# Two attention stages of a two-layer diffusion block rewritten as loops over cycles, with own rooms for weights and modulation loads

## The chip, the cores and the metric

The kernel runs on one core of one Trainium2 chip. TensorE (PE) multiplies matrices, VectorE (DVE), ScalarE (ACT) and GpSimd (POOL) work on rows of numbers, and SyncE (SP) issues most transfers. The metric is device microseconds (us) of one execution, as the median of several timed runs. Beside the timed runs there is one profiled execution with its trace; all views of the profile come from it.

## The reference, cut to what matters

Two trunk layers run on 256 context tokens and 512 latent tokens of width 1024, in fp32. Layer 0 mixes tokens by differential attention, layer 1 by neighbourhood attention with a learned bias. Each is followed by a squared-ReLU MLP, and each half is shifted, scaled and gated by six vectors of 1024 that come from `silu(c) @ w_mod`.

```python
for i in range(DEPTH):                                   # DEPTH = 2
    mod_l = split(silu(c) @ w_mod[i] + b_mod[i], 6)      # mod_c likewise from c_ctx
    h_l = modulate(rms_norm(x, norm1_g[i]), mod_l[0], mod_l[1])
    h_c = modulate(rms_norm(ctx, norm1_g[i]), mod_c[0], mod_c[1])
    # layer 0, 8 heads, two q/k maps of 64 each; latents read context + latents, context reads context
    #   s = q @ k.T / 8;  p = softmax(s);  w = p[map 0] - lam * p[map 1];  o = rms_norm(w @ v) * (1 - lam_init)
    # layer 1, 16 heads of 64; a latent reads the context and a window of 8 rows x 16 columns
    #   p = softmax([s_window + bias, s_context]);  o = p @ v
    x = x + mod_l[2] * (o @ w_o)
    x = x + mod_l[5] * (square(relu(modulate(rms_norm(x), mod_l[3], mod_l[4]) @ w_mlp1[i])) @ w_mlp2[i])
    # context tokens: the same with mod_c, in layer 0 only
```

## The kernel before, in words

The 768 tokens are six tiles of 128: tiles 0 and 1 are context, 2 to 5 latent. A product of two fp32 numbers is made of three passes over parts that are rounded to a shorter form (`PASSES`: high by high, and both mixed ones). So a weight that is loaded into a raw buffer `R` (two buffers, `wload`, L110) is first copied by ACT into the high half of a tile `W` (L118), and then POOL subtracts that from the raw value into the low half (L119). A matmul on `W` waits for both.

The stages follow each other on PE: a first head whose projection is merged with the first modulation chunks; layer 0's attention; its output projection; the MLP; layer 1's attention in eight groups of two heads; its output projection; the MLP. In an attention stage PE's instructions are not reordered: they stand as the text of the kernel issues them (`tc.manual_schedule`). The other engines and SP are ordered by a scheduler, each in a fixed order of its own, and every queue is worked off in that order.

**Layer 0's attention.** A head has these steps: the projection of six tiles, each in two half steps of twelve 128x384 matmuls (`qkv0`, L375); the turning of rope-rotated q and k (L453); scores (L499), softmax (L504, L505 and the blend L511), turning of the softmax weights (L523 and the copies L525, L526), the product with v (L534), and the turning of its output (L487, L488). Tables of letters, `ORD_HEAD` and its kind, say in which order generators are stepped: `q` the projection of the next head, `a` the attention of this one, `b` the first scores of the next, `z` the tail of the one before, `l`, `m` and `n` load, begin and end of a modulation chunk (eight 32x256 matmuls, L224, and a few small ones). At a head's end `b q a` puts two half steps of the last tile, the next head's scores of tile 0, and this head's last turn one behind the other. The first head of the loop runs by `ORD_HEAD0`, after a first head that is not in it. At its end `ORD_OUT0` weaves the last head's attention with the output projection over seven heads; the eighth follows whole (`while not last`).

**Rooms.** `sbuf_phase` opens a set of tile rooms that is closed as a whole: "s0" (five `W` of 1024 columns), "sA" (eight `W` of 768), "sB" (five of 1024) and so on. Modulation loads are two halves of 512 KB through `R` in the attentions, and one of 1 MB in a `W` room elsewhere. Of 48 chunks 8 are in the first head, 17 in layer 0's attention, 19 beside layer 0's MLP and 4 (`MODS_LATE`) in layer 1's attention.

**Layer 1's attention** is built alike: `qkv1` projects (L375), `attend1` does scores (L642), softmax, turning (L667) and product (L683), ordered by `ORD_FIRST1`, `ORD_GROUP`, `ORD_GROUP7` and `ORD_OUT1`. The projection of a group runs beside the attention of the one before; the first group's projection stands alone at the start.

Of the kernel before, what the change touches and what calls it, by code (L numbers as in the profile page):

```python
# [35 lines left out]
ORD_HEAD0 = "l qqqq a q a q a m aa q n a q aa q a l a q aa m aa q n aaa q a q aa b q a"  # L36
ORD_HEAD = "a q z a q z aa q z p q l a q aa q m l q a q a n q aa m aa q n aa q aa qq aa b q a"
ORD_OUT0 = "l a z a m z a n z q l p a a m a a n q a a q aa l aa q m aa q aa q n aa q a qq a q a q a Q"
ORD_FIRST1 = "qqqqqqqqqqqq rr q r a"
ORD_GROUP = "q a qq a qq aa q a q aa q a q r a r q a r a b"  # L40
ORD_GROUP7 = "l q a qq a qq aa q a q aa q a q m a n q a a b"
ORD_OUT1 = "q a l a m a n l aa m a n q aa q a q a qq a l m n Q"

MODS_LATE = 4


ATT0 = ((0, 1), (1, 0), (2, 0), (1, 1), (2, 1), (0, 2), (3, 0), (0, 3), (1, 2), (3, 1), (2, 2), (0, 4), (1, 3),
        (3, 2), (2, 3), (0, 5), (1, 4), (3, 3), (2, 4), (1, 5), (2, 5), (3, 4), (3, 5))
ATT1 = ((0, 1), (1, 0), (2, 0), (0, 2), (1, 1), (2, 1), (0, 3), (1, 2), (2, 2), (1, 3), (2, 3))
# [9 lines left out]
class Block:  # L59
    def __init__(self, tc, ctx, a):  # L60
# [9 lines left out]
        self.room = {}  # L70


    BUFS = {"H": 8, "Q": 8, "E": 2, "X": 2, "Y": 6, "O": 4, "T": 2, "SQ": 12, "SA": 12, "SO": 8, "V": 1, "C4": 1}

    def sbt(self, tag, shape, dt=F32):
        self.n += 1
        pool, bufs = (self.room[tag], self.bufs[tag]) if tag in self.room else (self.sb, self.BUFS[tag])
        return pool.tile(shape, dt, tag=tag, name=f"{tag}{self.n}", bufs=bufs)

    @contextmanager  # L80
    def sbuf_phase(self, name, wcols, **tags):

        with ExitStack() as st:
            self.wcols, self.bufs = wcols, tags
            self.room = {tag: st.enter_context(self.tc.tile_pool(name=name + tag, bufs=n, reuse_waits="tile"))
                         for tag, n in tags.items()}
            yield
# [22 lines left out]
    def wload(self, src, n, tile=None, eng=None):  # L110
# [5 lines left out]
        if w is None:  # L116
            w = self.sbt('W', [P, 2, self.wcols], F32R)
# [213 lines left out]
    def first_head(self, xnT, mods):  # L331
# [8 lines left out]
        def modulate_pair(kp):  # L340
            for _ in range(2):
                mods.load(True)
            w[kp] = self.wload(self.a["wqa"][0, kp], 768)
# [368 lines left out]
    def project(self, l, wo, oT, last, t0, xsrc, tag_o, tag_h, tag_p, out):  # L712
# [43 lines left out]
        while not last:  # L756
            yield
# [308 lines left out]
```

## Time and profile before

| what | us |
|---|---|
| three timed runs | 2003.57, 1999.56, 2001.33 (median 2001.33) |
| profiled execution, its own time | 1994.66 |
| its span in the profile | 1992.5 |
| PE busy in the span | 1826.0 (92%) |
| DVE, ACT, POOL busy | 1174.4, 808.4, 793.1 (59%, 41%, 40%) |

By the trace the stages lie at these times from the span's start: the first head to 65.9 us, the first two heads of the loop to 205.4, the next four to 437.4, the last to 490.4, the end of layer 0's attention with the first part of its output projection to 577.5, the rest of that projection and layer 0's MLP to 1206.4, the first group of layer 1 to 1247.3, six groups to 1501.1, the last group with the first part of the output projection to 1595.3, and layer 1's MLP to the end.

The profile is read by stage. Its windows view has one row for a stretch: from and to, its length, then busy time and number of instructions of PE, PEld (weight loads of PE), DVE, ACT and POOL, then the clock that PE was granted (1.00 is full), the share of time in which the transfer engines were busy, and GB/s. A row of the timeline is a run of like instructions: start, length, engine, line, operation, output and inputs, shapes, count, and in brackets the idle time ahead of it and what ended it. A row of the chain of waits has start, length, engine and what ran.

### The profile page before, as it was taken

To read this page: it belongs to the slowest core of one execution; us is meant where nothing else is said; L and a number is where in the kernel's file an instruction comes from. 1 tells how busy PE (TensorE), PEld (TensorE's weight loads), DVE (VectorE), ACT (ScalarE), POOL (GpSimd) and SP (SyncE) were. 2 spreads that over 40 slices of the span, in tenths; PEclk is the share of its full clock that TensorE was granted. 3 is DMA by queue.
4 is the path that set the end of the run, shared out by engine and by line. 5 is a ranking of instruction groups with operands and counts; after the bars stand their busy time and mean duration, and the time that the engine had idled before them with its cause. 6 is when DMAs were issued, how large, how long until landed. Compare 5 with 4: busy or idle time off the path is not lost.

```text
span 1992.5 us, 27095 instructions
## 1 busy us (share of the span) xinstructions
PE 1826.0 (92%) x10256; PEld 1592.5 (80%) x10256; DVE 1174.4 (59%) x2191; ACT 808.4 (41%) x1819; POOL 793.1 (40%) x684
## 2 busy tenths in 40 slices
PE   6689888898889999999999988889897889999998
PEld 5678787887668888888899978888887678888886
DVE  4577767777656433433434686777778564444446
ACT  4465656566525212212222244555566342322231
POOL 3644545544422212222323444445443234443443
PEclk9799999999899999999999998999999889999999
DMA  7211211213523323323321132222323423332332
GB/s 292 70 54 67 83 67 61 83 43 125 167 74 117 98 93 127 127 92 125 112 64 64 52 102 69 54 54 62 75 61 122 138 75 95 96 106 85 95 97 72
DMA packets 59441, 185.00 MB, mean 93 GB/s; under 512 B 7408, under 2 KB 13872, under 8 KB 55856
## 3 DMA queue, kind: packets, MB, share of 16 engines
q1 hardware_dynamic: 53568, 173.44, 28.0%
q10 hardware_dynamic: 5744, 9.85, 1.3%
q8 instruction: 80, 1.31, 0.3%
q14 instruction: 49, 0.40, 0.1%
HBM read 174.45 MB, written 8.81 MB: 92 GB/s over the span
## 4 chain that ended last, share of the span: by engine, by line
PE 68%; DVE 15%; ACT 6%; DMA 4%; issue 4%; POOL 2%; SPq 0%; ACTq 0%; POOLq 0%; DVEq 0%
PE PD L800 21%; PE PA L375 11%; PE PA L835 10%; PE PB L835 9%; PE PA L729 4%; PE PS L499 2%; PE PA L224 2%; PE PB L534 2%; PE PB L683 1%; PE PQ L365 1%; DVE SA L504 1%; ACT E L505 1%; ACT W L118 1%; DVE N L278 1%; DMA R<-in_wqb_dram 1%
## 5 line engine op out<-in xcount | busy, mean ns | idle before, releaser
L119 POOL TENSOR_TENSOR W<-R,W 128x1024 fp32r<-128x1024 f32 (+1 forms) x200 | 452.0, 2268 | 686.3 <-ACT W L118 648.2
L118 ACT ACTIVATE W<-R 128x1024 fp32r<-128x1024 f32 (+1 forms) x204 | 199.7, 995 | 460.3 <-PE PB L835 357.1
L800 PE MATMUL PD<-Q,W 128*128 128x384 f32 (+1 forms) x1584 | 291.3, 334 | 1.2 <-DVE Q L300 0.7
L800 PEld LDWEIGHTS PD<-Q,W 128*128 128x128 f32 x1584 | 271.8, 188 | 13.4 <-issue 4.9
L375 PE MATMUL PA<-W,H 128*128 128x384 f32 x1008 | 210.7, 360 | 10.3 <-DVE Q L431 5.0
L375 PEld LDWEIGHTS PA<-W,H 128*128 128x128 f32 x1008 | 186.9, 203 | 16.2 <-issue 5.2
L809 DVE TENSOR_TENSOR N<-N 128x768 f32<-128x768 f32 (+1 forms) x64 | 63.6, 997 | 223.9 <-ACT N L805 117.6
L800 PE MATMUL PD<-H,W 128*128 128x512 f32 (+1 forms) x816 | 183.9, 382 | 3.4 <-DVE H L301 2.5
L800 PEld LDWEIGHTS PD<-H,W 128*128 128x128 f32 x816 | 149.2, 192 | 32.8 <-DVE H L301 2.7
L375 PE MATMUL PA<-W,Q 128*128 128x384 f32 (+1 forms) x1008 | 172.8, 325 | 2.2 <-ACT H L411 2.2
L835 PE MATMUL PA<-W,H 128*128 128x512 f32 x648 | 165.4, 395 | 3.0 <-DVE T L841 2.7
L375 PEld LDWEIGHTS PA<-W,Q 128*128 128x128 f32 x1008 | 159.1, 192 | 2.4 <-ACT H L411 2.4
L263 POOL TENSOR_TENSOR SQ<-SQ,half 128x4 f32<-128x4 f32 (+1 forms) x96 | 92.7, 968 | 167.9 <-DVE SQ L386 158.8
L835 PEld LDWEIGHTS PA<-W,H 128*128 128x128 f32 x648 | 119.4, 188 | 30.6 <-issue 4.5
L835 PE MATMUL PB<-W,H 128*128 128x512 f32 x504 | 129.6, 391 | 0.0
L835 PE MATMUL PA<-W,Q 128*128 128x512 f32 x432 | 110.4, 395 | 2.2 <-ACT Q L811 1.6
L835 PEld LDWEIGHTS PB<-W,H 128*128 128x128 f32 x504 | 94.3, 188 | 18.6
L499 PE MATMUL PS<-Q,Q 128*128 128x256 f32 (+1 forms) x320 | 72.2, 360 | 30.7 <-ACT E L505 27.4
L835 PEld LDWEIGHTS PA<-W,Q 128*128 128x128 f32 x432 | 81.2, 188 | 22.1 <-ACT Q L811 2.4
L846 DVE TENSOR_TENSOR H<-PA,H 128x512 f32<-128x512 f32 x78 | 53.6, 688 | 70.9 <-PE PA L835 70.9
L504 DVE TENSOR_REDUCE SA<-PS 128x1 f32<-128x768 f32 (+1 forms) x96 | 74.5, 776 | 27.9 <-PE PS L499 14.4
L505 ACT ACTIVATE E<-PS,SA 128x768 f32<-128x768 f32 (+1 forms) x96 | 72.8, 759 | 39.2 <-DVE SA L504 39.2
(218 smaller groups left out, 3144.9 us busy)
## 6 DMA issues: line engine op xcount, KB each, us to landing
R<-in_w_dram SPq DMA_DIRECT2D x128, 512.0 KB
W<-in_wmod_dram SPq DMA_DIRECT2D x27, 1024.0 KB
R<-in_wmod_dram SPq DMA_DIRECT2D x42, 512.0 KB
R<-in_wqa_dram SPq DMA_DIRECT2D x32, 384.0 KB
R<-in_wqb_dram SPq DMA_DIRECT2D x32, 384.0 KB
X<-in_rpb_dram SPq DMA_DIRECT2D x48, 128.0 KB
R<-in_woa_dram SPq DMA_DIRECT2D x8, 512.0 KB
R<-in_wob_dram SPq DMA_DIRECT2D x8, 512.0 KB
```

Of the source, the lines that this page charges most:

```text
L118: nc.scalar.activation(w[:, 0, :n], raw, AF.Copy)
L119: (eng or nc.gpsimd).tensor_sub(w[:, 1, :n], raw, w[:, 0, :n].bitcast(F32))
L263: nc.gpsimd.tensor_tensor(r, ss, self.half[:, :n], op=ALU.pow)
L375: nc.tensor.matmul(acc[:, :n], hT[kt][:, x, P * i:P * i + P], w[kt // 2][:, y, o:o + n], start=(kt == 0 and p == 0), stop=(kt == KT - 1 an ...
L499: nc.tensor.matmul(s[:, c0:c1], q[:, m, P * i:P * i + P], k[:, m, c0:c1], start=p == 0, stop=p == 1)
L504: nc.vector.tensor_reduce(mx, s, op=ALU.max, axis=AX, negate=True)
L505: nc.scalar.activation(e[:, m, :nk], s, AF.Exp, bias=mx[:, 0:1], accum_out=sm[:, m:m + 1])
L729: nc.tensor.matmul(ps, oHL[h][:, x, c:c + P], w[h // 2][:, y, 512 * (h % 2):512 * (h % 2) + 512], start=(first and h == hs[0] and p == 0), ...
L800: nc.tensor.matmul(ps[:, at:at + b1 - b0], w[kt // 4][:, x, o:o + P], hT[kt][:, y, b0:b1], start=(kt == 0 and p == 0), stop=(kt == KT - 1 ...
L809: nc.vector.tensor_mul(r, r, r)
L835: nc.tensor.matmul(ps, hd[:, x, P * i - c0:P * i - c0 + P], w[f][:, y, 512 * n:512 * n + 512], start=(f == 0 and p == 0), stop=(f == len(h ...
L846: nc.vector.tensor_add(av, ps, av)
```

## The change

Both attentions become loops over cycles. `head0` and `group1` return a function of a letter and a number: `Q` a projection step, `U` a turn of q and k, `S` scores, `T` the turning of softmax weights, `V` the product with v, `O` the turning of an output. A string per cycle says the order; a step without a mark is of head c, with one mark of head c-1, with two of head c-2. `run` reads it. The steps issue the operations that they issued before. In layer 0 the cycle of head c holds its projection, the attention of c-1 and the last products and outputs of c-2. `START0` weaves heads 0, 1 and 2; `END0` the rest of heads 6 and 7 with the output projection over six heads (`P`; `X` loads and splits the seventh), in two half steps of nine matmuls for a tile; heads 6 and 7 follow in `end`, six matmuls for a tile in place of three. In layer 1 the cycle of group c holds its projection and the attention of c-1.

```diff
-ORD_HEAD = "a q z a q z aa q z p q l a q aa q m l q a q a n q aa m aa q n aa q aa qq aa b q a"
+CYCLE0 = """Q0a O2'' n1' S1' O3'' V4'' V5'' U4' Q0b Q1a T0' T1' Q1b O4'' S2' V0' Q2a O5'' Q2b S3' T2' U0 Q3a V1' O0'
+Q3b S4' T3' Q4a Q4b V2' O1' m0 S5' T4' U2 n0 Q5a V3' Q5b m1 S0 T5'"""
+START0 = """Q0a' Q0b' Q1a' Q1b' Q2a' S0'' Q2b' S1'' Q3a' U0' T0'' Q3b' T1'' Q4a' V0'' V1'' Q4b' S2'' U2' Q5a' O0''
+S3'' T2'' Q5b' O1'' m0 Q0a V2'' S4'' T3'' n0 Q0b U4' O2'' V3'' S5'' T4'' m0 Q1a O3'' V4'' n0 Q1b S0' T5''
...
+END0 = """O2'' n1' S1' O3'' V4'' V5'' m0 T0' U4' T1' n0 O4'' V0' S2' O5'' P0a V1' X6 P0b O0' S3' T2' P1a O1' P1b
+S4' T3' P2a V2' P2b m1 S5' T4' P3a V3' O2' n1 P3b T5' P4a V4' O3' P4b V5' O4' P5a P5b O5'"""
-ORD_GROUP = "q a qq a qq aa q a q aa q a q a r q a r q a r a b"
+CYCLE1 = """Q0 S0' Q1 Q2a S1' T0' Q2b Q3a S2' T1' Q3b Q4a U0 V0' S3' Q4b Q5a T2' Q5b V1' T3' U2 V2' U4 V3'"""
+END1 = """S0' S1' T0' S2' T1' P2a V0' S3' P2b T2' P3a V1' P3b T3' P4a X6 V2' P4b P5a V3' P5b"""
-MODS_LATE = 4
@@ sbt: a tag with several rooms goes round over their buffers
+            pools = [r[:2] for r in self.room[tag] for _ in range(r[1])]
+            k = self.turns[tag] = self.turns.get(tag, -1) + 1
+            pool, bufs = pools[k % len(pools)]
@@ mod_load
-            w = self.sbt('W', [P, 2048])
+            w = self.sbt('M', [P, 2048])
@@ head0, the first head's tile step
-            eng = nc.vector if accs and i in (2, 4) else nc.gpsimd
+            eng = nc.vector if accs and i in (2, 4, 5) else nc.gpsimd
@@ head0, output(i): one tile and one transfer for two output tiles
-        if last is None:
-            nc.scalar.dma_start(self.oT0[h], oTs[0])
+            if i % 2 == 1:
+                if split:
+                    split(oTs[j], j)
+                else:
+                    nc.scalar.dma_start(self.oT0[h][:, 256 * j:256 * j + 256], oTs[j])
@@ project
-            split(st, nc.vector if h % 3 == 0 and h else nc.gpsimd)
+                split(h, nc.gpsimd if h % 3 == 2 else nc.vector)
@@ hybrid_block
+        mod = {"m": lambda _: (mods.begin(), mods.load(True)), "n": lambda _: mods.end()}
+        b.open("left", WA=4)
+        b.open("right", N=2, M=3)
...
+            b.close("M", "N")
+            b.open("right", M=1, O=4, OT=2, WB=4)
...
+            def after(h):
+                if h + 2 < HEADS0:
+                    w[h + 2] = b.load_qkv(a["wqa"], h + 2, ("WA", "WB")[h % 2])
+                elif h + 2 == HEADS0:
+                    b.close("WA")
+                    b.open("left", W=3)
+                    proj.update(b.project(0, a["woa"], b.oT0, 0, lambda i: xs[i], 'H', 'Q', 'S', done))
+                    for k in range(3):
+                        proj["weights"](k)
+                else:
+                    b.close("WB")
+                    b.open("right", N=4, W=1)
+                    proj["begin"]()
...
+                for c in range(2, HEADS0):
+                    heads[c] = b.head0(c, w[c], hT, split=proj.get("split_last"), then=lambda c=c: after(c))
+                    run(START0 if c == 2 else CYCLE0, c, heads, **mod)
@@ sideB, called twice in an iteration of layer 0's MLP
-                if len(mods.todo) > MODS_LATE:
-                    mods.load(True)
-                    mods.chunk()
+                mods.chunk()
+                mods.load(True)
@@ layer 1
-        ph.enter_context(b.sbuf_phase("sC", wcols=768, W=6, N=4))
+        b.open("left", W1=6)
+        b.open("right", VM=2, N=4)
...
+                for c in range(GROUPS1):
...
+                    run(CYCLE1, c, heads)
+                b.close("W1")
+                b.open("left", W=4)
```

`WA` holds the weights of even heads and `WB` those of odd ones, four tiles each; the load for head h+2 is issued behind head h's last projection step (`then`), into the same room. A modulation load in layer 0's attention and MLP is one transfer of 1 MB into the only buffer of `M`, issued behind the chunk that used it. The MLPs have four `W` in place of five. Of the 48 chunks 8 are in the first head, 16 in layer 0's attention (4 in `START0`, two in each of five cycles, 2 in `END0`), 24 beside layer 0's MLP and none in layer 1's attention.

The rows below show three places, first of the kernel before, then of the change. Each row is an instruction (or a run of like ones): the line, what it is, output, inputs and shape. The lines of `wload` are L118 and L119 before, L127 and L128 now.

PE at the end of a cycle of layer 0: `PS` are score banks, `PA` projection banks, `PB` banks in which softmax weights `E` are turned, `Q` the head's q and k, `H` the tokens.

```order
L499 MATMUL PS_2782<-Q_2206,Q_2204 128x256
L375 MATMUL PA_2741<-W_1500,H_460 128x384 x3
L375 MATMUL PA_2741<-W_1500,H_467 128x384 x3
L375 MATMUL PA_2741<-W_1505,H_549 128x384 x3
L375 MATMUL PA_2741<-W_1505,H_556 128x384 x3
L523 MATMUL PB_2826<-ident,E_2689 128x128 x3
L523 MATMUL PB_2832<-ident,E_2689 128x128 x3
L499 MATMUL PS_2860<-Q_2205,Q_2204 128x256
```

```order
L233 MATMUL PA_3463<-M_3323,silu 32x256 x8
L493 MATMUL PS_3478<-Q_3137,Q_3136 128x256
...
L517 MATMUL PB_3495<-ident,E_3325 128x128 x3
L517 MATMUL PB_3501<-ident,E_3325 128x128 x3
L384 MATMUL PA_3507<-WB_2772,H_321 128x384 x3
L384 MATMUL PA_3507<-WB_2772,H_328 128x384 x3
L384 MATMUL PA_3507<-WB_2777,H_374 128x384 x3
L384 MATMUL PA_3507<-WB_2777,H_381 128x384 x3
L545 MATMUL PB_3521<-ident,O_3302 128x128
L248 MATMUL PA_3463<-sel,T_3472 128x2 x2
L493 MATMUL PS_3529<-Q_3137,Q_3136 128x256
```

Before, the six turns of tile 5 stand between the scores of tile 0 (`PS_2782`) and of tile 1 (`PS_2860`) with nothing else; now a chunk's matmuls stand ahead of the first scores (`PS_3478`), and twelve projection matmuls of the next head, an output turn and the chunk's small matmuls between the turns and the second scores (`PS_3529`).

ACT at the start of the output projection: `E` are exponentials, the rows `H<-N` the copies of head outputs that come back from memory, `OT` (`N<-PB` before) the outputs of the last heads.

```order
L505 ACTIVATE E_5728,SA_5729<-PS_5730,SA_5739 128x768
L235 DMA gates<-T_5755 2x256
L721 ACTIVATE H_5627<-N_5625 128x768
L721 ACTIVATE H_5632<-N_5630 128x768
L505 ACTIVATE E_5728,SA_5729<-PS_5730,SA_5742 128x768
L721 ACTIVATE H_5642<-N_5640 128x768
L721 ACTIVATE H_5647<-N_5645 128x768
L721 ACTIVATE H_5657<-N_5655 128x768
L505 ACTIVATE E_5779,SA_5780<-PS_5781,SA_5790 128x768
```

```order
L519 ACTIVATE X_5548<-PB_5549 128x384
L519 ACTIVATE X_5548<-PB_5555 128x384
L717 ACTIVATE H_5480<-N_5478 128x768
L499 ACTIVATE E_5530,SA_5531<-PS_5532,SA_5537 128x256
L717 ACTIVATE H_5485<-N_5483 128x768
L546 ACTIVATE OT_5561<-PB_5562,subg 128x128
L717 ACTIVATE H_5490<-N_5488 128x768
L499 ACTIVATE E_5530,SA_5531<-PS_5532,SA_5540 128x256
L717 ACTIVATE H_5495<-N_5493 128x768
```

Before, the copies stand beside the exponentials of a latent tile (128x768); now they begin beside those of a context tile (128x256), one ahead of the first and two ahead of the second of its exponentials.

POOL between two groups of layer 1: `SQ` is the power for the norm of q and k, `X<-X,C` the bias with its mask, `H` copies of k, `VM` copies of v.

```order
L119 TENSOR_TENSOR W_11898<-R_11896,W_11898 128x768
L263 TENSOR_TENSOR SQ_12083<-SQ_12081,half 128x4
L119 TENSOR_TENSOR W_11903<-R_11901,W_11903 128x768
L572 TENSOR_TENSOR X_12878<-X_12878,C_6651 128x256
L119 TENSOR_TENSOR W_12403<-R_12401,W_12403 128x768
L572 TENSOR_TENSOR X_12878<-X_12878,C_6651 128x256 x5
L119 TENSOR_TENSOR W_12408<-R_12406,W_12408 128x768
L263 TENSOR_TENSOR SQ_12172<-SQ_12170,half 128x4
```

```order
L272 TENSOR_TENSOR SQ_12742<-SQ_12740,half 128x4
L573 TENSOR_TENSOR X_13178<-X_13178,C_6649 128x256
L128 TENSOR_TENSOR W_12390<-R_12388,W_12390 128x768
L573 TENSOR_TENSOR X_13178<-X_13178,C_6649 128x256
L128 TENSOR_TENSOR W_12395<-R_12393,W_12395 128x768
L573 TENSOR_TENSOR X_13178<-X_13178,C_6649 128x256 x2
L620 CAST VM_12874<-H_12423 64x256
L272 TENSOR_TENSOR SQ_12793<-SQ_12791,half 128x4
L128 TENSOR_TENSOR W_12895<-R_12893,W_12895 128x768
```

Between two powers (to `SQ_12172` before, to `SQ_12793` now) there stood three weight subtractions and six mask additions, and now stand two subtractions, four additions and a copy of v.

More of the change, by code (lines that the diff above doesn't have):

```diff
@@ L779, in mlp @@
+        return dict(weights=weights, begin=begin, split=split, step=step, split_last=split_last, end=end)
     def mlp(self, l, t0, xh, hT, tag, mid, done, side):
@@ L885, in chunk, with run @@
         self.end()
[L888 to L902 removed]
+def run(order, c, steps, **others):
+    for word in order.split():
+        kind, num, h = word[0], word[1:].rstrip("'"), c - word.count("'")
+        if kind in others:
+            others[kind](num)
+        elif h in steps:
+            steps[h](kind, 2 * int(num[0]) + (num[1:] == "b") if kind == "Q" else int(num))
 def hybrid_block(tc, a, out):
```

388 lines of the change are left out of this document (174 added, 214 removed).

## The prediction

> **What bounds the kernel now.** I read the page first, then the windows by stage, then PE's timeline and the chain of waits at the end of a head.
>
> ```profile
> span 1992.5 us, 27095 instructions
> PE 1826.0 (92%) x10256; PEld 1592.5 (80%) x10256; DVE 1174.4 (59%) x2191; ACT 808.4 (41%) x1819; POOL 793.1 (40%) x684
> ```
>
> PE bounds the whole, but 92% is a mean. The windows (from and to, length, busy PE, PEld, DVE, ACT, POOL, granted clock, transfer share, GB/s) show where it stands:
>
> ```profile
> 65.90:205.40 139.50, 108.97 (x639) 96.69 (x639) 99.25 (x205) 78.77 (x218) 79.10 (x93) 0.87 0.22 71
> 205.40:437.40 232.00, 204.88 (x1310) 187.23 (x1308) 167.03 (x379) 139.92 (x407) 114.21 (x152) 0.94 0.21 70
> 437.40:490.40 53.00, 50.12 (x341) 44.03 (x342) 38.58 (x95) 32.55 (x99) 22.44 (x35) 1.00 0.29 97
> 490.40:577.50 87.10, 67.73 (x329) 51.44 (x327) 55.61 (x100) 40.12 (x91) 33.29 (x23) 0.84 0.44 144
> 674.30:1004.20 329.90, 329.90 (x1848) 286.29 (x1849) 127.33 (x169) 70.84 (x91) 88.09 (x37) 1.00 0.34 113
> 1206.40:1247.30 40.90, 38.48 (x244) 38.00 (x243) 22.06 (x59) 17.46 (x52) 20.00 (x25) 0.94 0.23 53
> 1247.30:1501.10 253.80, 227.11 (x1549) 218.65 (x1550) 192.74 (x442) 149.20 (x395) 119.31 (x141) 0.98 0.25 61
> 1501.10:1595.30 94.20, 77.09 (x444) 60.43 (x442) 65.48 (x128) 45.57 (x102) 30.16 (x23) 0.87 0.42 135
> ```
>
> In the MLP (674.30) PE is never idle. In the attentions it stands, and at less than the full clock. Four heads take 232.00, so 58.0 each; the fifth takes 53.00 at clock 1.00 with 50.12 busy. The gap lies at a head's end (timeline, then two pieces of the chain, then a window):
>
> ```profile
> 376.12 2.55 DVE L511 SCALAR_TENSOR_TENSOR E<-E,SA 128x768 f32<-128x768 f32 x1
> 378.73 0.93 PE L523 MATMUL PB<-ident,E 128*128 128x128 f32 x6 [0.72 <-DVE E L511]
> 383.35 1.23 PE L499 MATMUL PS<-Q,Q 128*128 128x256 f32 x4 [3.69 <-ACT E L505]
> 438.72 0.74 PE L499 MATMUL PS<-Q,Q 128*128 128x256 f32 x4 [2.73 <-ACT E L505]
> 384.57 3.84 PE PA L375 x12
> 390.42 2.10 PE PA L375 x12
> 326.40:330.20 3.80, 3.80 (x13) 3.80 (x13) 3.52 (x8) 1.49 (x5) 2.98 (x3) 0.50 0.30 102
> ```
>
> The scores of tile 1 wait 3.69 until the exponentials of tile 0 have emptied the only score bank; behind that the next twelve matmuls take 3.84 in place of 2.10, and the window of the same place a head earlier has clock 0.50. After the wait of 2.73 the clock stays at 1.00 (window 437.40). So a head of 58.0 loses some 7 in waits and slow clock. The Trainium skill's "TensorE: Matmul & The Clock Gate", section "What's actually happening", has the clock at half or full, falling after an idle window of about 3.4 us; the two waits agree with it, and it would bring the penalty back with any wait that long.
>
> **The change, part by part.**
>
> *Steady cycles of layer 0.* The matmuls stay; their order moves. The work of a head at full clock is 50.12, less a third chunk that this window holds (1.00 + 0.55 by the two rows below, about 1.4 in it): 48.7. This is the floor of a cycle.
>
> ```profile
> 785.17 1.00 PE PA L224 x16
> 790.24 0.55 PE PA L230 x2
> 503.12 3.79 DMA R<-in_wmod_dram
> ```
>
> Between the scores of tiles 0 and 1 now stand twelve projection matmuls (2.10) and the turns, and ahead of tile 0's a chunk (1.00). The wait of 3.69 goes down to nearly nothing, and the half clock behind it with it (3.84 − 2.10 = 1.7). What is late next: the softmax of tile 5, whose blend L511 takes 2.55 where POOL's weight subtraction runs beside it, and ACT, which still has weight copies among the exponentials.
>
> ```profile
> L511 DVE SCALAR_TENSOR_TENSOR E<-E,SA x48: 473/1018/2551, 96.4 to 543.1; 128x768 f32<-128x768 f32 x32, 128x256 f32<-128x256 f32 x16
> L118 ACT ACTIVATE W<-R 128x768 fp32r<-128x768 f32 x60 | 49.7, 849 | 32.6 <-DMA R<-in_wqb_dram 22.0 <-DMA R<-in_wqa_dram 7.7 <-DVE SA L257 2.0
> L119 POOL TENSOR_TENSOR W<-R,W 128x768 fp32r<-128x768 f32 x60 | 110.7, 1849 | 48.6 <-issue 36.3 <-ACT W L118 12.2
> ```
>
> I leave 3.3 for waits per cycle, bounded by 0 (all hidden) and 9.3 (a head as slow as now); 3.3 is near the 2.9 that the 53.00 window idles, plus half of one weight copy (0.85). A cycle is 52.0; four of them gain 4 × 6.0 = 24.0. The fifth has 48.7 + 2.9 = 51.6, gain 1.4. The Trainium skill's "SBUF — State Buffer", section "Who interferes with whom", has a DVE instruction with two SBUF inputs and a GpSimd one that reads SBUF shut each other out; the 2551 against a median of 1018 agrees. By it the blend stays slow wherever a weight subtraction meets it, some 1.5 us a cycle, and the sum would be 6 less in gain.
>
> *Loads.* A chunk's load is now 1 MB, issued when the chunk before it has been used, since `M` has one buffer. The row above has 512 KB in 3.79, so two are 7.6. From `m0` to `m1`, the narrower window of a cycle, stand two half steps (2 × 2.10) and a set of scores, a product and two sets of turns, an estimate of 9 us with 1.5 to 1.7 for each of the first two; from `m1` round to `m0` the rest of the cycle, some 40. In the MLP the window at 674.30 holds nine iterations with two chunks' places each: 329.90/18 = 18.3, less the 1.00 of the matmuls, about 17.5. So 7.6 is hidden everywhere; without that cover each load costs what it is late by (the last rival). SP waits at this load, and the weight loads behind it wait too: those of head h+2 are issued a head ahead, in rooms of their own, so nobody stands for them. The per-pair output transfers (three for one) are on ACT's queue and small; 0.
>
> *Start.* Three heads merged replace two loop heads of 139.50. Its waits:
>
> ```profile
> 67.42 0.44 PE L375 MATMUL PA<-W,H 128*128 128x384 f32 x1 [1.51 <-ACT W L118]
> 70.01 3.94 PE L375 MATMUL PA<-W,H 128*128 128x384 f32 x11 [2.14 <-POOL W L119]
> 76.39 1.32 PE L375 MATMUL PA<-W,H 128*128 128x384 f32 x6 [1.63 <-POOL W L119]
> 80.55 1.11 PE L453 MATMUL PA<-ident,Y 128*128 128x128 f32 x4 [2.85 <-DVE Y L445]
> 92.25 0.66 PE L453 MATMUL PA<-ident,Y 128*128 128x128 f32 x2 [3.79 <-ACT W L118]
> 98.16 4.18 PE L375 MATMUL PA<-W,H 128*128 128x384 f32 x12 [3.97 <-DVE Q L431]
> ```
>
> Two cycles of work with their residue are 2 × 52.0 = 104. The waits for weights (1.51 + 2.14 + 1.63 = 5.3) come before any attention can fill them and stay. Of the other three (10.6) half stays, since the rope of tile 5 moves to DVE and more heads are there to weave: 5.3. For slow clock I add 3. Together 118, gain 21.5 (bounds: 5, with all waits as before, to 35, with none).
>
> *End of layer 0's attention.* 87.10 now.
>
> ```profile
> 577.47 14.16 PE L729 MATMUL PA<-W,H 128*128 128x512 f32 x61 [0.37 <-DVE T L734]
> 508.98 5.62 DMA N<-oT
> ```
>
> A matmul of 128x512 is 14.16/61 = 0.232. Twelve half steps of nine are 25.1, the last two heads' 36 are 8.4 (18 more than before), and a cycle without its projection (144 matmuls of 2.10/12, 25.2) is 23.5: work of 57. The copies of the six heads' outputs now stand among the exponentials of tile 0 and 1 on ACT, and each waits for its transfer (5.62 for one): I put 6 there, 3 at the first half steps, 7 for small waits and clock, 16 in all (bounds 6 and 30; 19.4 idle now). 73, gain 14.1.
>
> *Layer 1.* The three windows are 40.90 + 253.80 + 94.20 = 388.9. First group:
>
> ```profile
> 1352.83 3.09 PE L375 MATMUL PA<-W,Q 128*128 128x256 f32 x24
> 1223.13 8.69 PE L375 MATMUL PA<-H,Q 128*128 128x384 f32 x48
> ```
>
> its projection is 48 × 0.129 + 96 × 0.181 = 23.6, with turns 24.2, and 4 for waits: 28. Then seven cycles:
>
> ```profile
> 1289.70:1332.00 42.30, 37.03 (x260) 35.68 (x260) 32.39 (x75) 25.16 (x68) 20.70 (x24) 1.00 0.25 63
> 1358.48 1.97 PE L683 MATMUL PB<-N,H 128*128 128x256 f32 x8 [2.56 <-DVE N L670]
> 1365.81 0.33 PE L595 MATMUL PA<-ident,Y 128*128 128x128 f32 x1 [1.31 <-DVE Y L388]
> L572 POOL TENSOR_TENSOR X<-X,C 128x256 f32<-128x256 f32 x48 | 37.3, 788 | 34.7 <-DMA X<-in_rpb_dram 32.4 <-DVE Q L300 2.3
> L263 POOL TENSOR_TENSOR SQ<-SQ,half 128x4 f32<-128x4 f32 x80 | 81.7, 1021 | 164.5 <-DVE SQ L386 155.9 <-DVE E L652 6.1 <-DVE SA L508 1.3
> L388 DVE SCALAR_TENSOR_TENSOR Y<-Y,SQ 128x256 f32<-128x256 f32 x80 | 50.6, 633 | 17.1 <-POOL SQ L263 16.7
> ```
>
> The work is 37.03; 5.3 is idle, the 2.56 largest. The new order puts two more steps ahead of the product that waited 2.56. What is late next is the last turn (`U4`): ahead of tile 5's power POOL has two weight subtractions, four mask additions and a copy of v: 2 × 1.85 + 4 × 0.79 + 1.02 + 0.63 = 8.5, with about 0.5 for the copy 9.0, against 6.8 of PE work: 2.2 late. With 0.8 at the first scores and 1.0 for the rest a cycle is 41.0 (bounds 37.0 and 42.3), seven are 287. The end is work of 37.03 − 23.6 = 13.4 (attention) + 96 × 0.232 = 22.3, so 35.7, with 12 of waits (bounds 5 and 17): 48. In all 363, gain 25.9, four chunks that leave included.
>
> *MLP of layer 0.* Five more chunks (24 for 19) of 1.00 + 0.55, and a tenth for the gaps around them: 1.66 each, −8.3, since PE has no idle time there to take them in. Four `W` for five: a weight tile has a whole phase (14 us) from its release to its use, and one copy and subtraction are under 4; 0. The first head's rooms: its loads set its pace and are the same; 0.
>
> Sum: 24.0 + 1.4 + 21.5 + 14.1 + 25.9 − 8.3 = 78.6. The profiled execution has 1994.66 (2.2 outside the span), so 1916.1; the median of the runs is 6.67 above it: **1923**.
>
> **Rivals.**
>
> *No waits in the cycles.* Layer 0's cycles run at 48.7 (4 × 3.3 + 2.9 = 16.1 less) and layer 1's at 38.0, its work and the 1.0 of small waits (7 × 3.0 = 21 less), start and end as forecast: 37 more gained, 1886. For it speaks the MLP, where PE never stands. Against it: weight copies on ACT still stand among the exponentials, and each POOL subtraction (1849) ahead of a power holds up a turn.
>
> *DVE sets the pace.* Woven closer, DVE is needed more densely. If it never gets beyond the 73% of the 437.40 window (38.58 of 53.00), a cycle with 41.76 of DVE takes 57, the start 136, the end 76, a cycle of layer 1 42.3 as now (28 + 296 + 52 in all): a gain of 4 + 0 + 3.5 + 11 + 13 − 8.3, about 23, 1978. Against it stands a stretch where DVE has 80% and PE does not wait:
>
> ```profile
> 350.00:360.00 10.00, 9.99 (x76) 8.69 (x76) 8.02 (x18) 5.74 (x16) 3.30 (x7) 1.00 0.30 95
> ```
>
> *The single modulation buffer stalls PE: slower.* The load starts only after the chunk before it, and PE's matmuls in fixed order stand behind the next. 31 chunks have windows of 9 (five), 12.5 (two) and 17.5 us (24 in the MLP). With a landing of t, the loss is the sum of t less its window: it eats the 78.6 from 31t = 568.6, t = 18.3 us. If the load waits behind others for 20 us, 11 × 5 + 7.5 × 2 + 2.5 × 24 = 130 are lost: 2053. For it: transfers are bunched, 0.34 of the time in the MLP. Against it: 7.6 by the row above.
>
> **How the numbers follow.** Forecast 0.70, all waits gone 0.07, DVE 0.12, single buffer 0.08, and 0.03 that gains and new waits cancel. The forecast's own range: the distances to the bounds are, faster and slower, 13 and 24 for the cycles, 13.5 and 16.5 for the start, 10 and 14 for the end, 28 and 9 for layer 1's cycles, 7 and 5 for its end; they will not all fall to one side, and their squares added give 35 either way: 1888 to 1958. The range that is to hold eight in ten reaches to the first two rivals, with 4 and 2 us (the runs shown lie 4 apart): 1882 to 1980. About 0.2% (4 us) can be told from no change; faster 0.89, same 0.03, slower 0.08.
>
> **What would show it.** In the profile after: windows of a layer-0 cycle near 52 with clock 1.00; no wait over 3 us ahead of L493; the chunk's matmuls (L233) not released by a transfer; the copies L717 between the exponentials at the end with a wait of PE's scores; a wait of about 2 at the last turn of a layer-1 group; the MLP 8 longer and PE full. The forecast is wrong if waits only change places at the head's end, or if L233 waits for `M`.

## The result, and the profile after

The changed kernel takes 1965.86 us (median of four runs, 1962.14 to 1968.20) where the kernel before takes 2000.44 (1998.78 to 2003.57): a ratio of 0.982 with an interval of 0.980 to 0.984. That is 34.6 us less, where 78.6 were forecast; 1965.86 lies in the stated range but beyond the forecast's own 1888 to 1958. The profiled execution took 1968.20, its span is 1966.4, against 1992.5 before. The pair of profiles thus shows 26.1 us of the 34.6: the profiled execution of before was 5.8 under its median, this one 2.3 over.

The page of the changed kernel, in the same two lines as before:

```profile
span 1966.4 us, 27084 instructions
PE 1814.6 (92%) x10256; PEld 1590.5 (81%) x10256; DVE 1146.6 (58%) x2204; ACT 813.3 (41%) x1822; POOL 798.0 (41%) x674
```

The means do not show where the time went: PE's share is 92% as before. So I measured the two traces from one event to the next, the same events in both: the start of the idle time ahead of the loop's first projection, the second scores (tile 1) at a head's end, the first matmul of each later stage.

| stretch | before | after | change | forecast |
|---|---|---|---|---|
| to the loop's first projection | 65.9 | 66.8 | +0.9 | 0 |
| start, to the second scores of the first steady boundary | 143.9 | 133.2 | −10.7 | −21.5 |
| five cycles, to the second scores at the last boundary | 281.9 | 261.0 | −20.9 | −25.4 |
| end of layer 0's attention, to the first MLP matmul | 120.5 | 106.6 | −13.9 | −14.1 |
| layer 0's MLP, to layer 1's first projection | 594.2 | 604.3 | +10.1 | +8.3 |
| layer 1's attention, to the first matmul of its MLP | 413.6 | 421.9 | +8.3 | −25.9 |
| rest | 372.5 | 372.6 | +0.1 | 0 |

The first two forecasts were cut some 4 us earlier than here; their sum of 46.9 against 31.6 is what can be compared. All of this is from one profile of each kernel, and stretches of one profile scatter: in the kernels below that leave them as they are, the start takes 133.2 to 137.2, layer 0's MLP 602.1 to 604.3 and layer 1's attention 416.9 to 421.9. The windows of the changed kernel (columns as in the prediction) show the same: the start, three cycles of layer 0, its end, the greater part of layer 1 and one cycle of it.

```profile
66.80:199.70 132.90, 105.07 (x642) 91.87 (x641) 94.90 (x216) 79.39 (x227) 74.02 (x89) 0.91 0.20 69
199.70:252.40 52.70, 47.84 (x326) 43.83 (x326) 39.33 (x93) 35.27 (x101) 33.54 (x41) 1.00 0.23 74
252.40:304.90 52.50, 49.29 (x327) 45.50 (x326) 39.61 (x93) 34.67 (x101) 31.57 (x39) 0.97 0.24 83
357.40:408.70 51.30, 47.52 (x327) 43.89 (x326) 40.63 (x96) 33.48 (x100) 27.15 (x35) 1.00 0.22 77
461.00:567.00 106.00, 98.78 (x495) 79.79 (x496) 69.05 (x141) 44.34 (x111) 25.69 (x23) 0.93 0.26 91
1205.00:1510.00 305.00, 265.98 (x1757) 259.85 (x1758) 211.56 (x508) 170.73 (x445) 126.42 (x154) 0.92 0.23 53
1248.80:1294.50 45.70, 38.71 (x258) 37.62 (x258) 30.48 (x74) 25.67 (x67) 20.28 (x25) 0.91 0.25 59
```

A cycle of layer 0 takes 51.3 to 52.7, forecast 52.0. A cycle of layer 1 takes 45.7 with clock 0.91, forecast 41.0, and was 42.3 with clock 1.00 before. PE's timeline at a head's end of layer 0, and at the last boundary:

```profile
252.69 0.73 PE L493 MATMUL PS<-Q,Q 128*128 128x256 f32 x4 [0.26 <-ACT E L499]
258.86 0.44 PE L475 MATMUL PC<-ident,Y 128*128 128x128 f32 x2 [2.23 <-POOL Y L457]
461.03 1.23 PE L493 MATMUL PS<-Q,Q 128*128 128x256 f32 x4 [3.09 <-ACT E L499]
```

The second scores wait 0.26 where they waited 3.69. What waits in their place is the last turn of q and k, 2.23, for tile 5's rope on POOL (L457).

### The profile page after: what moved, and what is told of

Read it like the earlier page. It is cut to its first block, busy times and chain, and to the rows that moved or that the text cites. A ratio compares the mean times of both kernels' runs of the same rounds, so it can differ in the third digit from the quotient of the medians.

```text
span 1966.4 us, 27084 instructions
## 1 busy us (share of the span) xinstructions
PE 1814.6 (92%) x10256; PEld 1590.5 (81%) x10256; DVE 1146.6 (58%) x2204; ACT 813.3 (41%) x1822; POOL 798.0 (41%) x674
## 4 chain that ended last, share of the span: by engine, by line
PE 68%; DVE 12%; POOL 6%; ACT 5%; DMA 5%; issue 3%; SPq 0%; ACTq 0%; POOLq 0%; DVEq 0%
PE PD L806 21%; PE PA L384 12%; PE PA L841 10%; PE PB L841 9%; PE PA L724 4%; DMA X<-in_rpb_dram 2%; PE PA L233 2%; POOL W L128 1%; PE PS L493 1%; PE PB L528 1%; PE PS L633 1%; DVE SA L498 1%; DMA R<-in_wqb_dram 1%; PE PB L678 1%; POOL SQ L272 1%
## 5 line engine op out<-in xcount | busy, mean ns | idle before, releaser
L128 POOL TENSOR_TENSOR W<-R,W 128x1024 fp32r<-128x1024 f32 (+1 forms) x168 | 397.3, 2374 | 613.3 <-ACT W L127 612.9
L127 ACT ACTIVATE W<-R 128x1024 fp32r<-128x1024 f32 (+1 forms) x172 | 171.9, 1023 | 476.5 <-PE PA L841 193.6
L806 PE MATMUL PD<-Q,W 128*128 128x384 f32 (+1 forms) x1584 | 297.6, 336 | 1.2 <-DVE Q L309 0.9
L384 PEld LDWEIGHTS PA<-W,Q 128*128 128x128 f32 x1008 | 164.4, 199 | 0.0
L841 PEld LDWEIGHTS PA<-W,H 128*128 128x128 f32 x648 | 119.6, 188 | 30.3 <-issue 4.5
L841 PE MATMUL PB<-W,H 128*128 128x512 f32 x504 | 124.0, 392 | 0.0
L384 PE MATMUL PA<-WB,H 128*128 128x384 f32 x576 | 114.1, 351 | 3.9 <-DVE Q L443 3.9
L384 PEld LDWEIGHTS PA<-WB,H 128*128 128x128 f32 x576 | 103.1, 196 | 5.5 <-DVE Q L443 5.0
L841 PEld LDWEIGHTS PA<-W,Q 128*128 128x128 f32 x432 | 81.1, 188 | 23.4 <-POOL W L128 3.1
L841 PE MATMUL PB<-W,Q 128*128 128x512 f32 x336 | 87.4, 395 | 0.0
L384 PE MATMUL PA<-WA,H 128*128 128x384 f32 x432 | 84.4, 346 | 1.0 <-DVE Q L443 1.0
```

The lines of the kernel that those rows point to most:

```text
L127: nc.scalar.activation(w[:, 0, :n], raw, AF.Copy)
L128: (eng or nc.gpsimd).tensor_sub(w[:, 1, :n], raw, w[:, 0, :n].bitcast(F32))
L384: nc.tensor.matmul(acc[:, :n], hT[kt][:, x, P * i:P * i + P], w[kt // 2][:, y, o:o + n], start=(kt == 0 and p == 0), stop=(kt == KT - 1 an ...
L806: nc.tensor.matmul(ps[:, at:at + b1 - b0], w[kt // 4][:, x, o:o + P], hT[kt][:, y, b0:b1], start=(kt == 0 and p == 0), stop=(kt == KT - 1 ...
L841: nc.tensor.matmul(ps, hd[:, x, P * i - c0:P * i - c0 + P], w[f][:, y, 512 * n:512 * n + 512], start=(f == 0 and p == 0), stop=(f == len(h ...
```

## The experiments

The theory: layer 1's cycle is set by the last turn of q and k (`U4`), which waits for tile 5's power in POOL's queue. By cover I mean the work that PE has between the step that feeds a chain on the other engines and the step that needs its end. In the changed kernel the rows of PE, POOL and DVE around it are:

```profile
1294.52 0.47 PE L611 MATMUL PA<-ident,Y 128*128 128x128 f32 x1 [5.29 <-DVE Y L397]
1294.85 1.95 PE L678 MATMUL PB<-N,H 128*128 128x256 f32 x8
1517.57 0.33 PE L611 MATMUL PA<-ident,Y 128*128 128x128 f32 x1 [0.29 <-DVE Y L397]
...
1285.43 1.82 POOL L128 TENSOR_TENSOR W<-R,W 128x768 fp32r<-128x768 f32 x1
1287.21 0.72 POOL L573 TENSOR_TENSOR X<-X,C 128x256 f32<-128x256 f32 x1
1287.90 1.82 POOL L128 TENSOR_TENSOR W<-R,W 128x768 fp32r<-128x768 f32 x1
1289.68 1.41 POOL L573 TENSOR_TENSOR X<-X,C 128x256 f32<-128x256 f32 x2
1291.39 1.01 POOL L272 TENSOR_TENSOR SQ<-SQ,half 128x4 f32<-128x4 f32 x1
...
1285.60 0.42 DVE L395 TENSOR_REDUCE SQ<-sq 128x4 f32<-128x260 f32 x1
1293.42 1.04 DVE L397 SCALAR_TENSOR_TENSOR Y<-Y,SQ 128x256 f32<-128x256 f32 x1
```

The sum of squares is there at 1286.02, the power starts at 1291.39: two weight subtractions, three mask additions and a copy stand ahead. The last group, which loads no weights for a next one, waits 0.29, and its cycle is 41.1 (from 1476.48, the turn before, to 1517.57). Five runs ask whether that is the cause.

**The mask additions left out.** Without them the bias of layer 1 has no mask, so this kernel computes less.

```diff
-            for j in range(3):
-                nc.gpsimd.tensor_add(b[:, m, j], b[:, m, j], self.mask[:, j])
```

> Leaves out the six mask additions of a group of layer 1 on POOL (six times 0.72, so the bias has no mask); all else as in the changed kernel. Theory (POOL's queue ahead of tile 5's power): four of the six stand there, 2.9 us and their waits for the bias transfers, so the wait at the last turn falls from 4.5 to about 1.5, the clock stays full, a cycle is about 41.5, the execution about 1943. Rival (the wait belongs to PE's order or to the weights' arrival, not to POOL's queue): waits of 4 to 5 stay, a cycle of 45.

Measured in one run: 1941.62 us; layer 1 takes 397 where the changed kernel has 422.

```profile
1317.23 1.73 PE L676 MATMUL PB<-N,H 128*128 128x256 f32 x8 [2.65 <-DVE N L663]
1323.87 0.33 PE L609 MATMUL PA<-ident,Y 128*128 128x128 f32 x1 [0.57 <-DVE Y L397]
```

From the second cycle on the turn waits 0.3 to 1.3 in place of 3.3 to 5.3, as the theory has it; a cycle is 42.4, as now a product waits 2.65 for its weights.

**Layer 1's weight subtractions on DVE.**

```diff
-                        w[c + 1] = b.load_qkv(a["wqb"], c + 1, "W1")
+                        w[c + 1] = [b.wload(a["wqb"][c + 1, s], 768, tag="W1", eng=nc.vector) for s in range(4)]
```

> Layer 1's weight subtractions move from POOL to DVE; all else as in the changed kernel. Theory (POOL's queue ahead of tile 5's power holds two subtractions of 1.82): the wait at the last turn falls from 4.5 to about 1, as in the last group, which has none (0.29); a cycle is 41.5 to 42.5, since DVE is 0.7 busy and takes four more, the execution 1945 to 1950. Rival (it is the bias transfers that hold POOL's queue, through the mask additions): the wait falls by under 1, a cycle of 44.5 or more.

Measured in one run: 1950.18, layer 1 406. The wait at the turn is gone from the second cycle on, but a cycle is 42.7 to 45.1, where 41.5 to 42.5 was expected, since PE now waits for DVE's part of the softmax weights (L665):

```profile
1326.50 1.12 PE L663 MATMUL PB<-ident,E 128*128 128x128 f32 x4 [4.25 <-DVE N L665]
...
1322.80 2.75 POOL L573 TENSOR_TENSOR X<-X,C 128x256 f32<-128x256 f32 x4
1322.85 2.99 DVE L397 SCALAR_TENSOR_TENSOR Y<-Y,SQ 128x256 f32<-128x256 f32 x1 [2.03 <-POOL SQ L272]
1326.56 0.41 DVE L395 TENSOR_REDUCE SQ<-sq 128x4 f32<-128x260 f32 x1
1327.06 1.73 POOL L272 TENSOR_TENSOR SQ<-SQ,half 128x4 f32<-128x4 f32 x1
```

So it is POOL's queue, by two different pieces taken out of it: here tile 5's power starts at 1327.06, 0.1 behind its sum of squares, where it started 5.4 behind. The wait of 4.25 is not a full DVE (36.10 busy in the 44.60 of this cycle): a scaling (L397, median 0.42 in this run) takes 2.99 while POOL runs four mask additions, and the softmax weights stand behind it on DVE (from 1325.77). In the cycle before, the moved subtraction itself holds DVE up: it waits 2.57 for its weight copy (ACT L127).

**The turn moved back, first try.** PE's order alone.

```diff
-CYCLE1 = """Q0 S0' Q1 Q2a S1' T0' Q2b Q3a S2' T1' Q3b Q4a U0 V0' S3' Q4b Q5a T2' Q5b V1' T3' U2 V2' U4 V3'"""
+CYCLE1 = """Q0 V3'' Q1 U4' Q2a S0' Q2b Q3a S1' T0' Q3b Q4a U0 S2' T1' Q4b V0' Q5a S3' T2' Q5b V1' U2 T3' V2'"""
```

> Layer 1 only, a new order of PE's steps: a group's last turn (U4) and last product (V3) move into the next group's cycle, behind its first two projection steps (3.09 us each), and the scores one step later. Theory (the turn waits for tile 5's power, which stands in POOL's queue behind weight subtractions and mask additions, and the cover between the last projection step and the turn is too short): the wait of 3.3 to 5.3 at the turn falls under 1, the half clock behind it goes, a cycle falls from 45.2 to about 41, the median from 1966 to about 1940. Rival (the queue on POOL is as long wherever the turn stands, and the scores of the next group then wait for the same keys): a wait of 3 to 4 ahead of the first scores, a cycle of 44 to 45, 1960 to 1966.

Measured: 1973.33, ratio 0.988 (0.986 to 0.990): slower than the changed kernel. The wait at the turn is gone, and two others are there:

```profile
1287.86 1.97 PE L678 MATMUL PB<-N,H 128*128 128x256 f32 x8 [3.44 <-DVE N L665]
1304.82 0.84 PE L633 MATMUL PS<-H,H 128*128 128x256 f32 x2 [2.80 <-ACT H L420]
```

The rival was right on the scores (2.3 to 2.8 for the keys of that turn, with one half step between); and my own order put a product (`V2'`) too close behind its turn of weights: 3.4 to 4.0. A cycle is 47.

**The turn moved back, with covers for what follows.** Two half steps between the turn and the scores, and one more ahead of each product.

```diff
+CYCLE1 = """Q0 V3'' Q1 U4' Q2a Q2b S0' Q3a S1' Q3b T0' S2' Q4a T1' U0 V0' Q4b S3' T2' Q5a V1' Q5b T3' U2 V2'"""
```

> Layer 1 again, with the last turn and the last product two projection steps into the next cycle, and now two half steps between that turn and the first scores, and a half step more between a turn of weights and its product. Theory (each step needs a cover as long as its chain: about 9 us for the turn, 3 to 4 for the keys, 5 for a product): no wait over 1.5, full clock, a cycle of 40 to 42, the median about 1940. Rival (a place where DVE or ACT is the bound: whatever PE's order, 3 to 4 us of waits stay in a cycle): 44 to 46, 1960 to 1970.

Measured: 1937.47 (1934.54 to 1940.12), ratio 0.970 (0.967 to 0.973). Two cycles and what is left at the turn:

```profile
1210.90:1250.70 39.80, 37.66 (x258) 35.55 (x258) 32.94 (x75) 25.80 (x66) 20.14 (x25) 1.00 0.29 67
1250.70:1292.40 41.70, 38.08 (x258) 35.58 (x258) 33.32 (x75) 25.80 (x67) 20.21 (x25) 1.00 0.28 64
1283.30 0.33 PE L611 MATMUL PA<-ident,Y 128*128 128x128 f32 x1 [1.24 <-DVE H L599]
```

39.8 and 41.7 at clock 1.00, layer 1 in 391 against 422. With the same work on POOL and DVE the wait of 3.3 to 5.3 is down to at most 1.6: what decided is how much of PE's work stands between a step and the step that needs it. The rival, that DVE or ACT bound the cycle, falls: DVE is at 83% of the first window.

**Layer 1's attention as before**, with layer 0 as changed and all 24 chunks beside layer 0's MLP.

```diff
-                for c in range(GROUPS1):
-                    ...
-                    run(CYCLE1, c, heads)
+            run_whole(mods, ORD_FIRST1, q=qkv, r=nqkv, a=att)
+                    ...
+                    run_whole(mods, ORD_GROUP if nqkv else ORD_GROUP7, q=qkv, r=nqkv, a=att, b=att2)
```

> Undoes the change in layer 1's attention alone: its generators, letter tables and out-projection as in the kernel before, with all 24 chunks still beside layer 0's MLP; layer 0 as changed. By the two profiles layer 1's attention (first projection to the second MLP) took 413.6 us before and 421.9 now; less the four chunks (6.6) the old code needs 407: the median falls from 1966 by about 15, to 1951. Rival (the forecast's step: the loop gains there, and the loss is elsewhere): slower by 10 to 20, 1976 to 1986.

Measured: 1964.80, ratio 0.983 (0.981 to 0.986): no difference from the changed kernel that the runs can tell, where 15 were expected. By its profile layer 1 takes 414.5, 7.4 less than in the changed kernel, but as much as before the change (413.6), when it also had the four chunks. That does not make the four free. Before, they stood beside the last group and its output projection (1522 to 1582), and from the same matmul on to the MLP that part is 6.9 shorter without them (window of the kernel before, then of this one):

```profile
1501.12:1620.01 118.89, 101.75 (x553) 80.56 (x552) 79.74 (x153) 54.23 (x121) 37.02 (x28) 0.89 0.36 116
1475.53:1587.49 111.96, 96.30 (x481) 81.51 (x480) 75.56 (x149) 52.78 (x117) 35.97 (x28) 0.86 0.27 86
```

What it gained there was lost ahead of it: the first group takes 45.4 where it took 40.9, and the six groups 257.1 for 253.8. In the first group four weight subtractions, in two pairs, stand ahead of powers that the turns need (before, one pair at 1214.67):

```profile
1179.20 3.66 POOL L135 TENSOR_TENSOR W<-R,W 128x768 fp32r<-128x768 f32 x2
1185.00 3.77 POOL L135 TENSOR_TENSOR W<-R,W 128x768 fp32r<-128x768 f32 x2 [1.47 <-ACT W L134]
1189.81 0.33 PE L725 MATMUL PA<-ident,Y 128*128 128x128 f32 x1 [1.89 <-DVE Y L404]
```

So this run does not bring the old stage back as it was. Each figure is from one profile; in the kernels with the changed loop the end of the stage scatters by less than 2.

**Layer 0's last turn a half step further back.**

```diff
-... V4'' V5'' U4' Q0b Q1a T0' T1' ...
+... V4'' V5'' Q0b U4' Q1a T0' T1' ...
```

> Layer 0 only: in a cycle the last turn of the head before (U4) moves one projection half step (2.1 us) further back. Theory (it waits 2.2 to 3.2 for tile 5's rope on POOL): the wait falls to 0.2 or less in five cycles, a cycle from 52.5 to about 50.4, the median from 1966 to about 1956. Rival (the wait moves to the scores of tile 2, which need the keys of that turn): 0.5 a cycle, 1963 to 1966.

Measured: 1959.87, ratio 0.982 (0.980 to 0.984), not to be told from the changed kernel's 0.982. In its trace the cycles from the second on are 50.2, 50.3, 51.0 and 52.1 (51.6 to 52.5 before the edit), the first three near the 50.4 expected. But the first of all is 54.7, since its turn still waits 3.00, and layer 0's attention as a whole is 496.7 for 500.7 (498.9 to 502.6 in the kernels that leave it as it is). From the second cycle on the scores of tile 2 now wait:

```profile
210.64 0.44 PE L475 MATMUL PC<-ident,Y 128*128 128x128 f32 x2 [3.00 <-POOL Y L457]
268.05 1.01 PE L493 MATMUL PS<-Q,Q 128*128 128x512 f32 x2 [0.92 <-ACT Q L420]
```

**The start.** Here the turns of the first head wait (rows of PE, then POOL and DVE, changed kernel):

```profile
80.71 0.66 PE L475 MATMUL PA<-ident,Y 128*128 128x128 f32 x2 [3.72 <-DVE Y L457]
87.59 0.69 PE L475 MATMUL PA<-ident,Y 128*128 128x128 f32 x2 [6.22 <-POOL Y L457]
...
75.62 3.81 POOL L128 TENSOR_TENSOR WA<-R,WA 128x768 fp32r<-128x768 f32 x2
...
75.97 3.60 DVE L453 TENSOR_TENSOR Y<-Y,C 128x128 f32<-128x128 f32 x2
87.85 0.49 DVE L453 TENSOR_TENSOR Y<-Y,C 128x128 f32<-128x128 f32 x2
```

Two products of tile 2's rope take 3.60 beside two weight subtractions of head 2, and 0.49 later.

First tile 5's rope was put back on POOL:

```diff
-            eng = nc.vector if accs and i in (2, 4, 5) else nc.gpsimd
+            eng = nc.vector if accs and i in (2, 4) else nc.gpsimd
```

> The start alone: tile 5's rope of the first head goes back from DVE to POOL; all else as changed. Theory of the forecast (the move of that rope shortens the start): the turns of the first head wait 2 to 4 longer in all, 1968 to 1970. Rival (the waits of 3.72 and 6.22 there are POOL's tile 3 and its weight subtractions, which stand ahead of it): no change or 1 to 2 less, 1964 to 1966.

Measured in one run: 1967.86, waits of 3.72 and 6.46. A difference of 2 is no more than single runs scatter (the kernel before ran in 1993.76 to 2002.39 beside it), and the two waits are as they were; the rope's engine does not explain them.

Then head 2's weights were loaded behind head 1's eighth half step:

```diff
...
-            after(0)
+            w[2] = []
...
+                heads[1] = b.head0(1, w[1], hT, then=lambda: after(1), begun=lambda: w[2].extend(b.load_qkv(a["wqa"], 2, "WA")))
```

> The start alone: head 2's weights are loaded behind head 1's eighth projection half step in place of ahead of all, so that their four copies and subtractions (7.3 on POOL) leave the turns of the first head. Theory (POOL's queue ahead of tile 3's rope, which stands behind three of these subtractions, makes the wait of 6.22 and part of 3.72): both fall by 5 to 7 together, the execution to about 1960. Rival (the turns wait for their own chain, powers and ropes of six tiles): 1965 to 1967; and if the weights then come late, a wait at the first projection of head 2.

Measured in one run: 1965.44, waits of 3.71 and 6.46. But the trace shows the subtractions where they were (from 75.89): the scheduler orders POOL, and it put them in the same place. The run says nothing on the theory.

Then the four subtractions were moved to DVE, and with them, in a second kernel, also tile 3's rope:

```diff
+                    w[h + 2] = [b.wload(a["wqa"][h + 2, s], 768, tag=("WA", "WB")[h % 2], eng=nc.vector if h == 0 else None)
+                                for s in range(4)]
```

> The start alone: head 2's four weight subtractions move from POOL to DVE; all else as changed. Theory (in the changed kernel two of them run on POOL from 75.6 to 79.4 while two DVE multiplications of tile 2's rope take 3.61 in place of 0.49, and what stands behind them on both engines is late): the rope takes about 0.5, the waits of 3.72 and 6.22 at the first head's turns fall by 3 to 6 together, the start from 132.9 to about 128, the execution to about 1961. Rival (the turns wait for their own chains of power and rope): both waits stay within 1 us, 1965 to 1967.

> The start alone: head 2's four weight subtractions and also tile 3's rope of the first head on DVE; all else as changed. With the subtractions alone moved, the turn of tile 3 still waited 4.63 for its rope on POOL, and the start ended no earlier. Theory (POOL's share of the first head is what the start waits for): the waits at the first head's turns fall from 13.4 to under 8, the first 38 us of the start by 5, the execution to about 1958. Rival (the first head's chain, six tiles of copy, square, sum, power, scaling and rope, ends no earlier whichever engine takes a piece of it): DVE is now the one that PE waits for, 1961 to 1965.

Measured in one run each: 1963.15 and 1962.41. Rows of the first, then of the second:

```profile
74.02 0.49 DVE L453 TENSOR_TENSOR Y<-Y,C 128x128 f32<-128x128 f32 x2
82.97 0.69 PE L475 MATMUL PA<-ident,Y 128*128 128x128 f32 x2 [4.63 <-POOL Y L457]
102.76 1.05 PE L475 MATMUL PC<-ident,Y 128*128 128x128 f32 x4 [4.36 <-POOL Y L457]
```

```profile
81.70 0.41 PE L475 MATMUL PA<-ident,Y 128*128 128x128 f32 x2 [3.68 <-DVE Y L457]
86.57 0.66 PE L475 MATMUL PA<-ident,Y 128*128 128x128 f32 x2 [4.46 <-DVE Y L457]
```

The rope's products are back at 0.49, so the collision is shown; but the turns still wait, and the start, from the loop's first projection to the second scores, takes 134.9 and 133.3, against 133.2 in the changed kernel and up to 137.2 in kernels with the same start. Some 5 us were expected there, and no gain can be told: what was freed at one wait came back at the next (4.36 at 102.76, where the changed kernel waits 3.16). That fits the second rival, a chain of six tiles that ends no earlier whichever engine takes a piece; it is not proved by it, and what would shorten the start stays open.

**Three edits together**: the order of layer 1 with covers, layer 0's turn, and head 2's subtractions on DVE.

> Three edits together: layer 1's last turn and product moved into the next cycle with longer covers, layer 0's last turn a half step further back, head 2's weight subtractions on DVE. If the waits are independent the gains add: 28 of the first, 3 to 10 of the second, 4 of the third from 1966, so 1924 to 1931. Rival (waits freed at one place come back at the next, above all in layer 0): 1933 to 1938, as with the first edit alone.

Measured: 1936.49, ratio 0.970 (0.968 to 0.972): the rival's case, no better than the first edit alone. Both beat the changed kernel by 25 to 29 us (by the ratios, and by the medians).

## Why the prediction was right or wrong

**Right: the waits at a head's end in layer 0, in part by luck.** The second scores wait 0.26 in place of 3.69, and a cycle is 51.3 to 52.7 where 52.0 stood. The residue of 3.3 had the right size and the wrong place: I put it on the blend L511 (now L505, which takes at most 1.4) and on ACT's weight copies; it is the wait of the last turn for the rope on POOL, 2.2 to 3.2 in four of the five cycles. That the sum came out is luck, since this wait was not in it. The gain of the five cycles is 20.9 for 25.4, some of it because the cuts differ.

**Right: the end of layer 0's attention** (−13.9 for −14.1), with the scores waiting 3.09 where I had put 6.

**Right: five more chunks in the MLP**, +10.1 for +8.3 (+7.9 to +10.1 over the profiles of all the kernels with this MLP), so 1.6 to 2.0 a chunk. The rival of the single modulation buffer falls: in the list of what PE's L233 waited for, no transfer stands, and the largest sum, 8.9, is time that waits for nothing that the profile shows.

```profile
L233 PE MATMUL PA<-M,silu x768: 379/379/404, 26.2 to 1041.1; 128*32 128x256 f32 x192
  issue: 8.9, 38
```

**Wrong: layer 1's cycle, the step "2.2 late" at the last turn.** Layer 1's attention is 34.2 of the 52.5 that the profiles lack (78.6 − 26.1; forecast −25.9, measured +8.3); of these, 25 lie in the seven cycles (from 1205.23 to 1517.57, 312.3 where 287 stood), some 5 in the first group (33.3 for 28) and some 4 behind them. The mechanism was named; the term was mis-sized. I counted POOL's queue against 6.8 of cover, 9.0 in all. The cover was 6.4 (the last projection ended at 1282.8, PE stood from 1289.2), and the chain took 11.7, to 1294.52: 3.2 of copy, square and sum (to 1286.02), 5.4 of what was left of POOL's queue, 1.0 of power, 1.0 in which DVE was held by another step's keys (L419, which wait for ACT), and 1.04 of scaling. The first and the fourth were not in my sum, which let POOL's queue of 7.4 start at once, and the scaling stood there with 0.63. The wait was 5.29 in this cycle, 3.3 to 5.3 in the second to seventh. Behind it, not in my sum at all, the clock falls, so that 37.0 of work becomes 38.71. Two turns of softmax weights wait 1.7 more, so 7.0 in all is idle: 37.0 + 1.7 + 7.0 = 45.7. That the order with its short covers is the cause, and not the loop, is shown by the run with covers: 39.8 and 41.7 a cycle, 391 for layer 1, near the 388 that the forecast comes to (363 and the 24.7 from there to the MLP).

**Open: the four chunks that leave layer 1.** They were counted as part of the gain there. In the run with the old layer 1 the part where they had stood is 6.9 shorter, so 1.7 a chunk, about what each costs in the MLP. By these two profiles the move neither gained nor lost; what it did in the new loop no run shows.

**Wrong: the start, 118 forecast, 132.9 measured.** Its work is 97.4 (two cycles). I left 17 for waits (5.3 for weights, 5.3 for turns, 6.6 of residue) and 3 for the clock; the trace has 28 of waits, and 7.7 more of busy time than the work at full clock (105.07 for 97.4; clock 0.91). The failed step is that half of the turns' waits would be filled: the first head's turns alone wait 3.72 + 6.22 + 1.53 = 11.5 where 5.3 stood. They run ahead of the loop, with four half steps of projection ahead of them; why they are not filled is not shown. Its first 38 us have PE busy for 20.86, and 23.48 with subtractions and rope on DVE (window of the changed kernel, then of that one):

```profile
66.80:105.00 38.20, 20.86 (x105) 18.86 (x104) 27.32 (x63) 18.95 (x57) 25.49 (x29) 0.78 0.16 52
66.80:105.00 38.20, 23.48 (x113) 22.10 (x114) 28.15 (x73) 18.82 (x55) 17.20 (x21) 0.79 0.16 50
```

**The rivals.** DVE as the bound is refuted for layer 0 (DVE 40.63 of 51.30 is 79%, above the 73% that I had taken as its limit) and for layer 1 by the run with covers. Its time was also added up wrongly: a fifth cycle of 57 against 53.00 loses 4 where I put 0, so 1982 and not 1978. "No waits in the cycles" was far off for the change as it is. None of the rivals gave the outcome; most of what is missing is the forecast's own mechanism with one term too small, and the start.

## What to carry to other kernels

When a hand-written order is changed, work out for each step its whole chain on the other engines, from the matmul that feeds it to the one that needs it (copies, sums, what stands ahead in each queue), and compare that with the work of PE in between: here 11.7 against 6.4 at one step took back the gain of the whole stage, and an order of the same steps with longer covers gave 25 to 28 us. A step moved away from its feeder is moved towards its user, so the user's cover has to be counted in the same go. A piece of work that is moved from POOL to DVE has to be checked against what POOL then runs beside it: here a scaling of 0.42 took 2.99 and a new wait of 4.25 stood behind it.

## What the runs showed of the hardware that was not expected

**DVE beside POOL.** Two products of 128x128 with both inputs from SBUF took 3.60 us while POOL ran two weight subtractions (75.62 to 79.43), and 0.49 without. The Trainium skill's "SBUF — State Buffer", section "Who interferes with whom", has such a pair exclude each other, the later one waiting for all of the earlier; the trace agrees, and the run that took the subtractions off POOL brought 0.49 back. In the run with layer 1's subtractions on DVE the scaling L397 took 2.99 beside mask additions, in the run without a mask 2.04 beside two weight subtractions.

**The clock.** PE's clock did not fall by the length of a single wait. After 5.29 eight matmuls took 1.95 where eight had taken 1.16 (row at 1294.85). But after a wait of 3.17 the next 3.4 us ran at full clock, and after one of 2.23 they did not:

```profile
207.18 0.44 PE L475 MATMUL PC<-ident,Y 128*128 128x128 f32 x2 [3.17 <-POOL Y L457]
207.20:210.60 3.40, 3.40 (x21) 3.40 (x22) 1.33 (x4) 1.49 (x4) 0.00 (x0) 1.00 0.00 0
258.90:262.30 3.40, 3.40 (x15) 3.40 (x16) 1.73 (x6) 1.21 (x4) 0.55 (x1) 0.71 0.00 0
```

So a forecast can't set the price of a wait of 2 to 3.5 by its length alone; why these two differ is not shown.
